# Hybrid attention, DeltaNet and PEER block: stores on the scalar engine's queue, three buffers for table rows, half of the gate columns made on VectorE, and dense rows pinned between the loop's steps

## The chip, the cores and the metric

The kernel runs on one core of a Trainium2 chip. The metric is device time in microseconds (us), the median of several executions. TensorE is called PE here, its weight loads PEld, VectorE DVE, ScalarE ACT, GpSimd POOL, and SyncE, which issues most transfers, SP.

## What is computed

One decoder layer on 512 tokens of width 1024: two mixers (sparse attention, gated DeltaNet), a merge, and then a retrieval layer (PEER) over 16384 single-neuron experts. The change touches only the PEER part, which the reference gives as:

```python
def peer(hn, w_query, sub_keys, u_tab, v_tab):
    q = (hf @ w_query).reshape(ntok, PEER_HEADS, 2, PEER_KEY_DIM // 2)
    s = jnp.einsum('nhpd,hpkd->nhpk', q.astype(f32), sub_keys.astype(f32))
    top_s, top_i = lax.top_k(s, PEER_TOPK)
    ...
    best_s, pos = lax.top_k(cand_s, PEER_TOPK)
    expert = jnp.take_along_axis(cand_i, pos, axis=-1)
    gate = jax.nn.softmax(best_s, axis=-1)
    ...
    def block(args):
        hb, eb, gb = args
        act = jax.nn.gelu(jnp.einsum('nhkd,nd->nhk', u_tab[eb], hb).astype(f32), approximate=False)
        coef = (gb * act).astype(hb.dtype)
        return jnp.einsum('nhk,nhkd->nd', coef, v_tab[eb])
```

Each token picks 8 x 16 = 128 experts of 128 x 128; for each it needs the product of its activation with a row of table u, a gelu, a gate, and a row of table v.

## The kernel before, in words

The program is written with a tile framework whose scheduler orders the instructions of each engine by a timeline of its own at build time; `tc.issue_after(ins)` (here `behind`, `held`) pins instructions of the same engine behind `ins`. Up to about 565 us the two mixers and the merge run, which the change leaves as they are. Then:

- **Scores and choice** (to about 832 us). Query projections and scores, then `choose(b)` for each of the four token blocks of 128, long runs of small DVE instructions that find the chosen experts and gates.
- **Dense u** (`dense_u(i)`, 128 table rows i of 128 experts each). For 320 of the 512 tokens (`NU`) the products with all experts are made: load `ut` (512 KB, two buffers), split it in a high and a low half (`uh` on ACT at line 174, `ul` on DVE at line 175), 24 matmuls of 128x320, and a gelu on ACT. The gelu's result stays in SBUF (`ge`, `AHEAD + 2` = 26 buffers) or, for the rows in `SPILLED` (60, set by `KEPT`), goes to DRAM (`gs`, line 836, issued by SP) and is loaded again later. 84 of the 128 rows (`first`: 24 kept ones and the 60 spilled) are made before the last loop, in step with the other work through `along`; the other 44 (`late`) in the last loop.
- **Gathered u and v**. Half of block 2 takes its u rows with 64 indirect DMAs of 512 KB (`ask`, line 977; product on DVE, line 992), and block 3 takes u and v rows with 128 indirect DMAs of 1 MB (`gathered`, line 998; product line 1006, sum into `x1g` line 1009). Both draw on the four `row` buffers.
- **Pieces** (`spread`, 24 pieces of 16 tokens, about 832 to 1152 us). For each token a matrix of gates over all experts is built as a product of two one-hot matrices: in two halves q of 8 tokens, DVE compares (`oa`, `ob`, line 1030), ACT scales each token's `ob` by its gates (line 1033, 8 instructions of 128x128), PE multiplies (two passes a token in the trace, 32 a piece), and ACT copies the sums of four tokens at a time into `gb` (line 1039). `gb` has one buffer of 1 MB and is stored to `gd` in DRAM (line 1041, issued by SP) in runs of 512 bytes.
- **The last loop** (`dense_v(i)` for 128 rows, about 1152 us to the end). Load `vt` (512 KB, two buffers), split it (`vh` on ACT, line 1127; `vl` on DVE, line 1128), multiply gates `gt` by the gelus (line 1131), split the product (`ch` on ACT, `cl` on DVE, two buffers each), and 18 matmuls of 128x512 that add to the accumulators `acc`. Gates for eight rows come in one load `gt` of 1.5 MB. About 120 of the gathers of block 3 are spread over the loop, paced by `vl`.

All matmuls stand under the helper's line 98, all splits under lines 174 and 175, all loads under line 109.

Of the kernel before, what the change touches and what calls it, by code (L numbers as in the profile page):

```python
# [19 lines left out]
P = 128  # L20
T = 512
D = 1024
# [26 lines left out]

AHEAD = 24  # L50
KEPT = 60
SPILLED = {i for i in range(P) if i * KEPT // P != (i + 1) * KEPT // P}

# [36 lines left out]
def tile_block(ctx, tc, x, xT, w_in, sc_cols, sc_rows, w_br, w_o, w_q, subT, uT, uv, cst, iota, out, dbg=None):  # L90
# [732 lines left out]
    def dense_u(i, a_):  # L823
        ut = up.tile([P, 8, P], F32, name="ut", bufs=2)
        load(ut, uT[i])
# [6 lines left out]
        if i in SPILLED:  # L832
            ge = up.tile([P, NU], F32, name="gs", bufs=2)
            gsd[i] = dr.tile([P, NU], F32, name=f"gs{i}")
            S.activation(ge, a_, AF.Gelu)
            nc.sync.dma_start(gsd[i], ge)
        else:
            ges[i] = up.tile([P, NU], F32, name="ge", bufs=AHEAD + 2)
            S.activation(ges[i], a_, AF.Gelu)
# [175 lines left out]
    def spread(b, gp):  # L1015
# [5 lines left out]
        for c in range(P // TC):  # L1021
            gb = gp.tile([P, P, TC], F32, name="gb", bufs=1)
            for q in range(TC // TB):
# [3 lines left out]
                ob = gp.tile([P, TB, P], F32, name="ob", bufs=2)  # L1027
                for i, o_ in enumerate((oa, ob)):
                    which = sl[:, i, n0:n0 + TB, None].to_broadcast([P, TB, P])
                    V.tensor_tensor(o_, io[:, None].to_broadcast([P, TB, P]), which, op=ALU.is_equal)  # L1030
                for t in range(TB):
                    n = n0 + t
                    S.activation(ob[:, t], ob[:, t], AF.Copy, scale=sl[:, 2, n:n + 1])  # L1033
                for g in range(TB // TG):
# [5 lines left out]
            dst = gd[:, :, b * (P // TC) + c, :].rearrange("g p k -> p g k")  # L1040
            nc.sync.dma_start(dst, gb.rearrange("p (g i) n -> p g (i n)", i=IC))
            yield
# [75 lines left out]
    def dense_v(i):  # L1118
# [3 lines left out]
        g = gts[i // IC][:, :, i % IC, :]  # L1122
        vt = ex.tile([P, D], F32, name="vt", bufs=2)
        load(vt, uv[i * P:(i + 1) * P, D:])
# [6 lines left out]
        V.tensor_tensor(gdn, activations(i).rearrange("p (c n) -> p c n", n=TC), gdn, op=ALU.mult)  # L1131
        ch = ex.tile([P, NCH, TC], F32R, name="ch", bufs=2)
        cl = ex.tile([P, NCH, TC], F32R, name="cl", bufs=2)
        split(ch, cl, g)
# [11 lines left out]
    for i in range(P):  # L1146
# [3 lines left out]
        if late and (total_u - len(late)) * (P - END) <= i * total_u:  # L1150
            dense_u(late.pop(0), ps3.tile([P, NU], F32, name="a_", bufs=2))
            spent += U_COST
# [73 lines left out]
```

## Time and profile before

| | |
|---|---|
| time, median of 3 runs | 1895.31 us (1889.37 to 1906.87) |
| profiled execution, its own time | 1899.46 us |
| its span, first to last instruction | 1897.7 us |
| mean granted TensorE clock | 0.98 of 2.4 GHz |
| busy, share of the span | PE 92%, PEld 80%, DVE 77%, ACT 48%, POOL 14% |
| moved by DMA | 433.77 MB, mean 229 GB/s |

The engines work side by side, so a busy share says little by itself. Matmuls are pipelined, and PE counts as busy while one is under way. What a stretch of the span is bound by is read from the chain of waits (which work ended last, followed back) and from what an engine waited for, stretch by stretch.

### The profile page before, as it was taken

Reading aid. Unit: us, or ns where it says so; the run is one execution under the profiler, and the core shown is the slowest. Engines: PE = TensorE matmul, PEld = TensorE weight load, DVE = VectorE, ACT = ScalarE, POOL = GpSimd, SP = SyncE. Lnnn points to the kernel's source line nnn. Section 1 sums busy time; section 2 is a strip of 40 time slices with the busy share of each in tenths; the row PEclk is TensorE's granted clock in tenths of the full one; section 3 lists DMA queues with packets and bytes.
Section 4 is the critical chain, followed back from the end, with each engine's and each line's share of the span. In section 5 each row is a group of like instructions: output and inputs, shape, how many; then the busy total and the mean of one; then the engine's idle time right before and its main releaser. Section 6 shows DMA issues by size and latency. Waiting matters only on the chain.

```text
span 1897.7 us, 26661 instructions
## 1 busy us (share of the span) xinstructions
PE 1754.7 (92%) x9527; PEld 1511.4 (80%) x9527; DVE 1463.5 (77%) x3084; ACT 912.4 (48%) x1787; POOL 270.8 (14%) x196
## 2 busy tenths in 40 slices
PE   6999999999999997888989898999999999789888
PEld 4787677777778897878988897888888888677666
DVE  5757988554766999988776776878878788789787
ACT  5533344434533343359977894434444443333333
POOL 0000000000000003430331102211111211222220
PEclk9999999999999999999999999999999999989999
DMA  4211111112633226877989799998989988989997
GB/s 148 85 68 67 45 45 58 60 45 85 210 128 122 79 103 258 296 244 217 298 282 310 248 291 334 359 356 320 346 329 337 343 333 319 349 329 359 343 343 254
DMA packets 155973, 433.77 MB, mean 229 GB/s; under 512 B 12480, under 2 KB 78144, under 8 KB 137408
## 3 DMA queue, kind: packets, MB, share of 16 engines
q1 hardware_dynamic: 128192, 264.28, 39.9%
q0 software_dynamic: 27648, 167.78, 23.8%
q8 instruction: 75, 1.23, 0.2%
q14 instruction: 58, 0.48, 0.1%
HBM read 388.73 MB, written 42.86 MB: 227 GB/s over the span
## 4 chain that ended last, share of the span: by engine, by line
PE 61%; DMA 15%; DVE 11%; ACT 8%; issue 4%; SPq 0%; DVEq 0%; ACTq 0%; POOL 0%; POOLq 0%
PE mm L98 21%; PE acc L98 19%; DMA vt<-in_uv_dram 6%; PE dn L98 5%; DMA gd<-gb 4%; PE wo L98 3%; DMA ut<-in_uT_dram 3%; PE at L98 3%; ACT gb L1039 3%; ACT ob L1033 2%; DVE ul L175 2%; DVE vl L1128 1%; ACT vh L1127 1%; DVE row L992 1%; ACT uh L174 1%
## 5 line engine op out<-in xcount | busy, mean ns | idle before, releaser
L98 PE MATMUL acc<-vl,ch 128*128 128x512 f32 x768 | 303.0, 395 | 2.3 <-DVE vl L1128 2.2
L98 PE MATMUL acc<-vh,cl 128*128 128x512 f32 x768 | 301.9, 393 | 0.0
L998 POOL DMA_INDIRECT row<-in_uv_dram,eidx x128 | 171.5, 1340 | 693.2 <-DVE x1g L1009 655.9
L98 PE MATMUL acc<-vh,ch 128*128 128x512 f32 x768 | 212.8, 404 | 42.5 <-ACT vh L1127 42.5
L98 PE MATMUL mm<-hTh,uh 128*128 128x320 f32 x672 | 217.9, 324 | 32.7 <-ACT uh L174 12.0
L98 PE MATMUL mm<-hTh,ul 128*128 128x320 f32 x672 | 218.4, 326 | 10.4 <-DVE ul L175 10.4
L977 POOL DMA_INDIRECT row<-in_uv_dram,eidh x64 | 99.1, 1548 | 901.0 <-DVE gate_g L913 730.0
L175 DVE TENSOR_TENSOR ul<-ut,uh 128x1024 fp32r<-128x1024 f32 x128 | 156.1, 1220 | 86.2 <-ACT uh L174 82.5
L98 PE MATMUL mm<-hTl,uh 128*128 128x320 f32 x672 | 214.3, 319 | 0.0
L98 PEld LDWEIGHTS acc<-vh,ch 128*128 128x128 f32 x768 | 144.5, 193 | 78.6 <-ACT vh L1127 51.2
L1128 DVE TENSOR_TENSOR vl<-vt,vh 128x1024 fp32r<-128x1024 f32 x128 | 156.4, 1223 | 50.6 <-ACT vh L1127 49.5
L174 ACT CAST uh<-ut 128x1024 fp32r<-128x1024 f32 x128 | 134.4, 1050 | 112.2 <-DMA ut<-in_uT_dram 51.0
L174 ACT CAST ch<-gt 128x384 fp32r<-128x384 f32 x128 | 65.6, 513 | 250.8 <-PE acc L98 246.6
L98 PEld LDWEIGHTS acc<-vl,ch 128*128 128x128 f32 x768 | 146.5, 191 | 34.7 <-DVE vl L1128 4.0
L98 PEld LDWEIGHTS acc<-vh,cl 128*128 128x128 f32 x768 | 145.8, 190 | 29.9
L1009 DVE SCALAR_TENSOR_TENSOR x1g<-row,co,x1g 128x1024 f32<-128x1024 f32 x128 | 163.8, 1280 | 5.5 <-ACT co L1008 3.5
L1127 ACT CAST vh<-vt 128x1024 fp32r<-128x1024 f32 x128 | 133.4, 1047 | 70.8 <-DMA vt<-in_uv_dram 70.1
L98 PEld LDWEIGHTS mm<-hTh,uh 128*128 128x128 f32 x672 | 131.5, 196 | 38.0 <-ACT uh L174 14.9
L1006 DVE CUSTOM_DVE_ANT_0 row<-row,h2g 128x1024 f32<-128x1024 f32 x128 | 154.6, 1219 | 0.9 <-DMA row<-in_uv_dram,eidx 0.9
L98 PE MATMUL mm<-hh,wh 128*128 128x512 f32 x344 | 144.6, 424 | 3.6 <-ACT hh L174 2.1
L98 PEld LDWEIGHTS mm<-hTh,ul 128*128 128x128 f32 x672 | 131.0, 195 | 13.2 <-DVE ul L175 13.1
L175 DVE TENSOR_TENSOR wl<-wt,wh 128x1024 fp32r<-128x1024 f32 (+1 forms) x81 | 90.1, 1115 | 63.5 <-ACT wh L174 63.2
(676 smaller groups left out, 3817.6 us busy)
## 6 DMA issues: line engine op xcount, KB each, us to landing
ut<-in_uT_dram SPq DMA_DIRECT2D x128, 512.0 KB
vt<-in_uv_dram SPq DMA_DIRECT2D x128, 512.0 KB
gd<-gb SPq DMA_DIRECT2D x24, 1024.0 KB
gt<-gd SPq DMA_DIRECT2D x16, 1536.0 KB
wt<-in_w_in_dram SPq DMA_DIRECT2D x43, 512.0 KB
gs<-gs SPq DMA_DIRECT2D x120, 160.0 KB
wt<-in_w_q_dram SPq DMA_DIRECT2D x16, 512.0 KB
sgd<-tmp SPq DMA_DIRECT2D x16, 256.0 KB
```

The source lines that it names most:

```text
L98: hop[0] = PE.matmul(o, l, r, start=start, stop=stop).ins
L174: S.copy(hi, src)
L175: return V.tensor_tensor(lo, src, hi.bitcast(F32), op=ALU.subtract).ins
L977: G.indirect_dma_start(out=asked[s // 2][:, s % 2], out_offset=None, in_=uv2, in_offset=bass.IndirectOffsetOnAxis(ap=eidh[:, s:s + 1], axi ...
L992: V.tensor_tensor_reduce(r, r, h2d, 1.0, 0.0, op0=ALU.mult, op1=ALU.add, accum_out=act[:, s:s + 1])
L998: G.indirect_dma_start(out=row.rearrange("p t d -> p (t d)"), out_offset=None, in_=uv, in_offset=bass.IndirectOffsetOnAxis(ap=eidx[:, s:s ...
L1006: V.tensor_tensor_reduce(row[:, 0], row[:, 0], h2g, 1.0, 0.0, op0=ALU.mult, op1=ALU.add, accum_out=a)
L1009: V.scalar_tensor_tensor(x1g, row[:, 1], co, x1g, op0=ALU.mult, op1=ALU.add)
L1033: S.activation(ob[:, t], ob[:, t], AF.Copy, scale=sl[:, 2, n:n + 1])
L1039: S.copy(gb[:, :, at:at + TG].rearrange("p i n -> p n i"), v4(p_))
L1127: S.copy(vh, vt)
L1128: paced = V.tensor_tensor(vl, vt, vh.bitcast(F32), op=ALU.subtract)
```

## The change

Gelu results (`gs`) and gate pieces (`gd`) are stored by DMAs that ACT issues instead of SP. `ut`, `vt`, `ch` and `cl` get a third buffer; `AHEAD` falls from 24 to 16 (18 buffers of `ge`) and `KEPT` rises from 60 to 68, so 68 rows are spilled; 84 rows still precede the loop and 44 are in it. In the second half (q = 1) of each piece the scaled one-hot matrix `ob` is made by eight DVE instructions of 128x128 (compare and multiply in one), in place of one compare of 128x1024 on DVE and eight scalings on ACT. In the loop a late `dense_u` is pinned on PE behind the last matmul of the `dense_v` before it.

```diff
-AHEAD = 24
-KEPT = 60
+AHEAD = 16
+KEPT = 68
...
-        ut = up.tile([P, 8, P], F32, name="ut", bufs=2)
+        ut = up.tile([P, 8, P], F32, name="ut", bufs=3)
...
-            nc.sync.dma_start(gsd[i], ge)
+            nc.scalar.dma_start(gsd[i], ge)
...
-                for i, o_ in enumerate((oa, ob)):
+                for i, o_ in enumerate((oa, ob)[:2 - q % 2]):
                     which = sl[:, i, n0:n0 + TB, None].to_broadcast([P, TB, P])
                     V.tensor_tensor(o_, io[:, None].to_broadcast([P, TB, P]), which, op=ALU.is_equal)
                 for t in range(TB):
                     n = n0 + t
-                    S.activation(ob[:, t], ob[:, t], AF.Copy, scale=sl[:, 2, n:n + 1])
+                    if q % 2:
+                        V.tensor_scalar(ob[:, t], io, sl[:, 1, n:n + 1], sl[:, 2, n:n + 1], op0=ALU.is_equal, op1=ALU.mult)
+                    else:
+                        S.activation(ob[:, t], ob[:, t], AF.Copy, scale=sl[:, 2, n:n + 1])
...
-            nc.sync.dma_start(dst, gb.rearrange("p (g i) n -> p g (i n)", i=IC))
+            nc.scalar.dma_start(dst, gb.rearrange("p (g i) n -> p g (i n)", i=IC))
...
-        vt = ex.tile([P, D], F32, name="vt", bufs=2)
+        vt = ex.tile([P, D], F32, name="vt", bufs=3)
...
-        ch = ex.tile([P, NCH, TC], F32R, name="ch", bufs=2)
-        cl = ex.tile([P, NCH, TC], F32R, name="cl", bufs=2)
+        ch = ex.tile([P, NCH, TC], F32R, name="ch", bufs=3)
+        cl = ex.tile([P, NCH, TC], F32R, name="cl", bufs=3)
...
-            dense_u(late.pop(0), ps3.tile([P, NU], F32, name="a_", bufs=2))
+            with behind(hop[0]):
+                dense_u(late.pop(0), ps3.tile([P, NU], F32, name="a_", bufs=2))
```

Since the scheduler orders anew, other instructions move too. On ACT, in one of the later pieces, the order before was:

```order
L1033 ACTIVATE ob<-ob,sl 128x128 x8
L174 CAST uh<-ut 128x1024
L835 ACTIVATE gs<-mm 128x320
L1033 ACTIVATE ob<-ob,sl 128x128 x8
L1007 ACTIVATE co<-a 128x1
L1008 ACTIVATE co<-co,gate_g 128x1
L835 ACTIVATE gs<-mm 128x320
L1039 COPY gb<-wo 128x4x128
L174 CAST uh<-ut 128x1024
L1039 COPY gb<-wo 128x4x128 x3
```

and in the changed kernel, with line 1036 for the scalings, 1042 for the copies and 1044 for the store, it is:

```order
L1007 ACTIVATE co<-a 128x1
L1008 ACTIVATE co<-co,gate_g 128x1
L174 CAST uh<-ut 128x1024
L835 ACTIVATE gs<-mm 128x320
L1036 ACTIVATE ob<-ob,sl 128x128 x8
L836 DMA gs_10423<-gs 128x320
L174 CAST uh<-ut 128x1024
L835 ACTIVATE gs<-mm 128x320
L1042 COPY gb<-wo 128x4x128
L836 DMA gs_10507<-gs 128x320
L1042 COPY gb<-wo 128x4x128 x3
L1044 DMA gd<-gb 128x16x128
```

One of the two blocks of eight scalings is gone, a cast no longer stands between the copies, and three issues of stores stand in ACT's stream, one of them between the copies.

At the end of the pieces ACT's order before kept two dense rows behind the last copies, and after the change (the second fence) the last two pieces have no dense row beside them:

```order
L1039 COPY gb<-wo 128x4x128
L174 CAST uh<-ut 128x1024
L1039 COPY gb<-wo 128x4x128 x3
L174 CAST uh<-ut 128x1024
L835 ACTIVATE gs<-mm 128x320
L174 CAST uh<-ut 128x1024
L835 ACTIVATE gs<-mm 128x320
L174 CAST uh<-ut 128x1024
```

```order
L1044 DMA gd<-gb 128x16x128
L174 CAST uh<-ut 128x1024
L835 ACTIVATE gs<-mm 128x320
L1036 ACTIVATE ob<-ob,sl 128x128 x8
L836 DMA gs_10923<-gs 128x320
L1042 COPY gb<-wo 128x4x128 x4
L1044 DMA gd<-gb 128x16x128
L1036 ACTIVATE ob<-ob,sl 128x128 x8
L1042 COPY gb<-wo 128x4x128 x4
L1044 DMA gd<-gb 128x16x128
L174 CAST ch<-gt 128x384 x3
```

What moved is dense rows, from the end of the pieces to their front. Counted over DVE's order, 36 dense rows (`ul`) and 28 products of line 992 stand ahead of the first `oa` before, and 41 and 32 now.

In the last quarter of the loop, SP's loads before were all for `dense_v`:

```order
L109 DMA vt<-in_uv_dram 128x1024 x4
L109 DMA gt<-gd 128x3072
L109 DMA vt<-in_uv_dram 128x1024 x2
L109 DMA gs<-gs_9965 128x320
L109 DMA gs<-gs_10000 128x320
L109 DMA vt<-in_uv_dram 128x1024 x2
```

and now loads of dense rows (`ut`) stand among them:

```order
L109 DMA vt<-in_uv_dram 128x1024 x2
L109 DMA ut<-in_uT_dram 128x1024
L109 DMA vt<-in_uv_dram 128x1024
L109 DMA gs<-gs_10042 128x320
L109 DMA gs<-gs_10126 128x320
L109 DMA vt<-in_uv_dram 128x1024 x2
L109 DMA ut<-in_uT_dram 128x1024
```

So loads of dense rows moved to the end of the loop. Before, the dense rows of the loop were made in its first 68 iterations, with single matmuls between those of `dense_v`; now one block of 24 stands after every second or third `dense_v`, to the end of the loop.

## Rows read from the trace of the kernel before

**Rows 1.** Busy time of each engine in four stretches of the span (choice, pieces, first and second part of the loop): stretch, its us, busy us with the number of instructions, granted clock, mean busy share of the 16 DMA engines, GB/s.

```profile
675.00:832.00 157.00, 133.77 (x842) 128.65 (x841) 147.34 (x540) 59.40 (x83) 49.54 (x35) 0.95 0.68 241
849.00:1152.00 303.00, 270.56 (x1889) 263.53 (x1888) 223.32 (x248) 254.82 (x569) 59.15 (x36) 0.96 0.86 276
1152.00:1590.00 438.00, 432.68 (x2255) 380.19 (x2254) 352.55 (x456) 189.88 (x355) 86.11 (x65) 1.00 0.91 340
1590.00:1898.00 308.00, 261.75 (x1080) 207.96 (x1079) 250.72 (x336) 112.90 (x228) 68.79 (x51) 0.95 0.88 328
```

**Rows 2.** The chain that ended last, shares by line, in the stretches 675 to 832, 832 to 1152 and 1590 to 1898 us.

```profile
by line: DVE ul L175 18.2%; DMA ut<-in_uT_dram 12.5%; PE mm L98 11.6%; DVE row L992 8.9%; issue 6.2%; DMA row<-in_uv_dram,eidh 4.8%; DVE oh L945 3.0%; DVE bp L908 2.9%; DVE bp L911 2.8%; ACT uh L174 2.7%; DVE cr L909 2.4%; DVE oh L946 2.2%; 
...
by line: DMA gd<-gb 26.5%; ACT gb L1039 15.3%; PE mm L98 13.2%; ACT ob L1033 11.5%; DMA ut<-in_uT_dram 8.5%; issue 7.0%; PE wo L98 6.1%; ACT uh L174 3.7%; DVE ob L1030 1.8%; DVE oa L1030 1.4%; ACT gs L835 1.1%; DVE row L992 1.1%; DVE ul L17
...
by line: DMA vt<-in_uv_dram 34.8%; PE acc L98 25.0%; issue 8.1%; DVE vl L1128 8.1%; ACT vh L1127 5.8%; DVE x1g L1009 4.0%; DMA gt<-gd 3.5%; DVE row L1006 3.2%; DVE gt L1131 2.4%; DVE cl L175 2.0%; ACT ch L174 0.7%; DVE xs L1164 0.4%; DVE a 
```

**Rows 3.** Who waited for whom between 1590 and 1890 us: us in total, times, longest.

```profile
ACT ch L174 <- PE acc L98: 90.6, 47, 3.6
ACT vh L1127 <- DMA vt<-in_uv_dram: 55.0, 28, 5.6
...
PE acc L98 <- ACT vh L1127: 38.5, 19, 6.1
```

**Rows 4.** The same between 1160 and 1590 us.

```profile
PE acc L98 <- ACT vh L1127: 4.0, 2, 2.7
```

**Rows 5.** Pieces of the chain between 832 and 1152 us in order of time: start, us, what.

```profile
864.30 5.19 DMA gd<-gb
...
875.66 5.34 DMA gd<-gb
...
919.44 9.47 DMA gd<-gb
930.96 2.23 ACT ob L1033 x8
936.28 5.67 DMA gd<-gb
...
1131.95 7.37 DMA ut<-in_uT_dram
1141.17 2.02 ACT gb L1039 x2
1143.20 8.88 DMA gd<-gb
```

**Rows 6.** Instructions on the tiles gb and act: line, engine, operation, count, ns (least, median, most), first and last start.

```profile
L1039 ACT COPY gb<-wo x96: 992/1093/1176, 839.2 to 1142.1; 128x512 f32<-128x512 f32 x96
L1041 SPq DMA_DIRECT2D gd<-gb x24: 370/371/378, 849.3 to 1143.2; - x24
...
L109 SPq DMA_DIRECT2D act_up<-act x1: 5895/5895/5895, 1035.5 to 1035.5; - x1
```

**Rows 7.** Two stores of gb by length: busy times and DMA in the 5.2 us of the store at 864.3 and the 9.5 us of the one at 919.4 (columns as in rows 1).

```profile
864.30:869.50 5.20, 5.20 (x41) 5.20 (x40) 4.38 (x7) 4.78 (x12) 0.00 (x0) 1.00 0.83 232
...
919.40:928.90 9.50, 9.50 (x73) 9.50 (x72) 7.89 (x9) 7.16 (x21) 1.96 (x1) 1.00 1.06 362
```

**Rows 8.** What SP issued next after the stores of 909.2 and 1143.2 us: start, us that the issue took, line, transfer.

```profile
909.64 2.12 SPq L836 DMA_DIRECT2D gs<-gs  x1
...
1144.39 4.74 SPq L836 DMA_DIRECT2D gs<-gs  x1
```

**Rows 9.** ACT's groups between 832 and 1152 us: busy us, mean ns of one, idle before.

```profile
L174 ACT CAST uh<-ut 128x1024 fp32r<-128x1024 f32 x50 | 52.6, 1051 | 15.9 <-DMA ut<-in_uT_dram 12.6 <-PE mm L98 3.3
L835 ACT ACTIVATE gs<-mm 128x320 f32<-128x320 f32 x45 | 19.9, 443 | 5.5 <-PE mm L98 3.0 <-issue 2.5
```

**Rows 10.** DVE's groups between 675 and 1152 us (columns as in rows 9).

```profile
L175 DVE TENSOR_TENSOR ul<-ut,uh 128x1024 fp32r<-128x1024 f32 x84 | 102.3, 1219 | 65.7 <-ACT uh L174 65.4
L992 DVE CUSTOM_DVE_ANT_0 row<-row,h2d 128x1024 f32<-128x1024 f32 x64 | 76.0, 1219 | 2.3 <-DMA row<-in_uv_dram,eidh 2.3
...
L1030 DVE TENSOR_TENSOR ob<-io,sl 128x1024 f32<-128x1024 f32 x48 | 58.5, 1219 | 0.0
...
L992 DVE DVE_READ_ACCUMULATOR2_ANT act<- 128x1 f32 x64 | 5.2, 82 | 0.0
...
L927 DVE TENSOR_SCALAR t<-bp 128x128 int32<-128x128 int32 x4 | 0.9, 218 | 0.0
```

**Rows 11.** The only group of DVE instructions with a column of scalars as operand and a compare-like form that is near in shape, by tile acc: ns (least, median, most) over the three shapes.

```profile
L533 DVE TENSOR_SCALAR acc<-R,small x3: 352/411/470, 117.6 to 242.7; 128x256 f32<-128x256 f32 x1, 128x384 f32<-128x384 f32 x1, 128x512 f32<-128x512 f32 x1
```

**Rows 12.** Pieces of the whole chain in which PE runs without a wait: 26 passes of the pieces' matmuls, 30 of `dense_v`, 24 of `dense_u`.

```profile
1124.28 2.90 PE wo L98 x26
...
1305.04 6.85 PE acc L98 x30
...
1371.61 3.52 PE a__14245 L98 x24
```

**Rows 13.** Three windows of the loop (columns as in rows 1).

```profile
1400.00:1450.00 50.00, 50.00 (x262) 44.00 (x262) 40.31 (x52) 21.34 (x39) 8.46 (x8) 1.00 0.95 361
...
1600.00:1650.00 50.00, 43.72 (x189) 34.69 (x187) 43.30 (x58) 18.60 (x40) 16.16 (x11) 1.00 0.91 348
...
1850.00:1898.00 48.00, 39.02 (x162) 31.09 (x161) 34.56 (x44) 14.61 (x30) 4.72 (x3) 0.93 0.71 253
```

## The prediction

> **What bounds the kernel now.** I read first the busy time by stretch, then the chain of waits inside each stretch, then who waited for whom. The part up to 675 us is built in the same order before and after, apart from one dense row, and is left out. Three stretches remain.
>
> *Choice, 675 to 832 us:* DVE is busy 147 of 157 us [rows 1], and the chain runs mostly over DVE, but 12.5% of it, 19.6 us, is waiting for the load `ut` [rows 2].
>
> *Pieces, 832 to 1152 us:* no engine is full (PE 271, ACT 255 of 303 us, rows 1). The chain is a cycle through the single buffer `gb`: its store is 26.5% of it, the copies into it 15.3%, the scalings on ACT 11.5%, and `ut` loads 8.5%, that is 27 us [rows 2]. The 24 stores are issued from 849.3 to 1143.2 us, one per 12.8 us [rows 6]. A cycle is a store and then the copies: 5.19 us and 6.2 us from 864.30 to 875.66, 9.47 and 7.4 us from 919.44 to 936.28, the second with eight scalings (2.23 us) among the copies [rows 5]. Stores come short or long: during the short one all traffic is 232 GB/s, during the long one 362, so the long ones share the engines with other transfers [rows 7].
>
> *The loop, 1152 to 1898 us:* two halves with different limits. To 1590 PE is busy 433 of 438 us, and waits for `vh` only 4.0 us; from 1590 PE is busy 262 of 308 us, waits 38.5 us for `vh`, which waits 55 us for the load `vt`, and `vt` is 34.8% of the chain [rows 1 to 4]. The reason is that all late dense rows were made in the first half.
>
> **The change part by part.**
>
> *1. Choice: more goes into it.* The built order puts 41 dense rows and 32 products ahead of the first `oa` where 36 and 28 stood. On DVE, which bounds here, that is 5 x 1.219 + 4 x (1.219 + 0.082) = 11.3 us [rows 10]. PE's 5 x 3.52 = 17.6 us fit in its 157 - 134 = 23 idle us [rows 1, 12]. Against it stands the third `ut` buffer, which can take away at most the 19.6 us of waiting; I take half. Sum: +1.5 us, between -8 and +11.
>
> *2. Pieces.* What is taken from ACT: eight scalings a piece; one block of eight took 2.23 us in a row [rows 5], so 24 x 2.2 = 53 us of ACT's time. What is added: the issues of 24 `gd` and of some 45 `gs` [rows 9], by SP's 0.37 and 0.33 us [rows 6, 8] 24 us. DVE gets eight instructions a piece for one of 1.219 us. An operation with two columns of scalars isn't in the trace; the nearest at 128x128 with fixed scalars takes 218 ns, and one with a column 352 ns at twice the width [rows 10, 11], so 24 x (8 x 0.218 - 1.22) = 13 us, at most 24 x (8 x 0.352 - 1.22) = 38 us. I take 13, for the shape is the same; DVE's 223 busy us of 303 hide it. If the cover is gone, it costs the difference of the two, 25 us.
>
> The store was not late before: SP stood waiting, and the store of 1143.20 followed the last copy at once [rows 5]. So the move to ACT doesn't bring the store forward; it frees SP. Behind a `gd` the next issue took 2.12 and 4.74 us [rows 8], and a `ut` load issued at 1131.95 needed 7.37 us [rows 5]. Now `ut` no longer queues behind the store, but may run beside it, and so lengthen it towards the 9.5 us of a shared one.
>
> A new cycle is therefore: store 7.0 us (short 5.3, long 9.5; I take a value between them that leans to the short, as only about two loads of 0.5 MB come per cycle), 0.3 to release ACT, four copies of 1.093 and the issues 0.33 and 0.37 in ACT's stream: 5.1 us [rows 6, 8]. That is 12.4 us. ACT's other work in the cycle (two casts and two gelus 3.0, one block of scalings 2.2, an issue) is 5.6 us and lies under the store [rows 5, 9]. PE needs 2 x 3.52 + 32 x 2.90/26 = 10.6 us and is not the limit [rows 12]. Twenty-one such cycles make 260 us; the last two, without a dense row beside them, store alone: 5.3 + 0.3 + 4.8 = 10.4 us each, 21 us. Before, one cycle was far longer: the piece for which block 2's gates must be ready waited for `act_up`, whose issue took 5.9 us behind a `gd` [rows 6]; SP is now free there, and I charge 4 us for what is left. Sum: 260 + 21 + 4 = 285 against 293.9: -9 us. With short stores throughout it is 21 x 10.7 + 25 = 250, -44; with long ones throughout 21 x 14.9 + 25 = 338, +44. Both ends are unlikely, as the stores before were mixed; for the range I take half of each, -22 to +22.
>
> The Trainium skill, "DMA: Bandwidth & Descriptors", section "Issuing engines are not separate DMA queues", says that issuing from several engines saves only the sequencer's time, usually small. In this trace that time is not small behind a `gd` [rows 8]. By the rule the pieces would give nothing, and the sum below would be 9 us worse.
>
> *3. The loop.* What it must move: 128 `vt` and 42 `ut` of 512 KB, 16 `gt` of 1.5 MB, 68 `gs` of 160 KB, some 120 gathers of 1 MB, and 3.7 MB at the end: 67.1 + 22.0 + 25.2 + 11.1 + 122 + 3.7 = 251 MB (the sizes follow from the tiles' shapes). Before it was about 250 MB in 746 us by the rates of rows 1; the eight rows more that are spilled add 1.3 MB here and as much in the pieces. What PE must do: 128 x 18 passes at 6.85/30 us and 42 blocks of 3.52 us: 526 + 148 = 674 us [rows 12]. So, spread evenly, both need about 5.3 us an iteration, and which ends last is open. Moving dense rows to the second half fills PE's idle 46 us there; the third buffers of `vt`, `ch` and `cl` take off both waits of rows 3. The question is the rate. Half one, with `ut` and `vt` in SP's queue, reached 361 GB/s in its best window, half two 348 [rows 13], and half one's mean was 340 with PE full. I take 357, near the best, for all but the last 48 us, whose drain at 253 GB/s (12 MB) remains: (251 - 12)/0.357 + 48 = 718 us against 746: -28 us. With half two's 348 it is 735, -11. With PE as the limit it is 674 us and about 16 for start and end (estimate): 690, -56. The pin costs something too: before, single dense matmuls filled PE's gaps; a block of 3.5 us can't be cut. I take nothing for it, since the waits it would cover in half one were 4.0 us [rows 4], at most the 38.5 us of half two, which would bring the loop back to +10.
>
> The Trainium skill, same page, section "Specifications", gives about 358 GB/s as the limit of HBM for a core. By it the loop could not end below (251 - 12)/0.358 + 48 = 716 us, and the second rival below would be out. The trace has one window at 361 [rows 13], so the rule is borne out as to size, not as a wall.
>
> **Sum.** 1.5 - 9 - 28 = -35.5 us on the profiled 1899.5: 1864. That execution lay 4.2 us over the median, so 1860 for the median.
>
> **The rivals.**
>
> *ACT is held by its own stores (slower).* An issue behind a `gd` blocked SP for 2 to 4.7 us [rows 8]. Now the `gs` issue behind a `gd` is ACT's, and behind it stand the cast `uh`, which PE's next dense row waits for, and the copies. In the later pieces ten instructions lie between the two, over 4 us, and little is left of the block; in the first eleven only a cast and a gelu, 1.5 us. From a stall of about 1.5 us a cycle ACT's 5.6 us exceed the store of 7 and every further us is on the path. With 4.7 us in each of 23 cycles it is 23 x 3.2 = 74 us more, less where the store is long anyway; with that 74, choice at +11, and the loop at -11, 1899.5 + 11 - 9 + 74 - 11 - 4.2 = 1960; in half of the cycles 1923. Against it: SP's blocks of over 2 us came right behind the `gd`, and ACT comes later.
>
> *PE becomes the limit of the loop (much faster).* If the third `vt` buffer keeps the transfers busy as never before, the loop takes 690 us; with the pieces at -9 the time is 1832. For it: PE without waits for 400 us in half one. Against it: no window before went over 361 GB/s, and this needs 239/0.642 = 372.
>
> *The loop stays at the rate of half two, and the pieces give nothing (no difference).* 1.5 + 0 - 11 = -9.5: 1886. For it: the DMA share is 0.91 and 0.88 in both halves [rows 1], as if transfers, not buffers, set the pace.
>
> **How the numbers follow.** This kernel's measurement can tell about 1% from no change. Forecast 0.48, around 1860; PE-bound loop 0.16; no difference 0.23; slower 0.13. Faster by over 1% (under 1876) takes the second and nearly all of the first: 0.61; within 1% takes the third and the slow tail of the forecast: 0.27; slower by over 1%: 0.12, the first rival. The range, 1826 to 1897, holds the second and third cases and the bounds of the loop, and leaves the slow rival out.
>
> **What would show it.** Right: PE busy about equally in all windows of the loop, no wait of `vh` for `vt` above a few us, over 350 GB/s in its middle; store-to-store time of about 12.4 us in the pieces, 10.4 in the last two; first store some us later than before. Wrong: `gs` issues on ACT of several us and `uh` behind them; stores of 9 us throughout; PE waiting for `vh` all along the loop at 348 GB/s; DVE's new instructions over 0.3 us; a fall of the granted clock from 1.0 in the loop, where it is 1.00 and 0.95 now [rows 1].

## The result, and the profile after

The changed kernel takes 1846.97 us (median of 4 runs, 1843.05 to 1852.02), 0.9733 of the kernel before, with an interval of 0.968 to 0.9785 (the four runs of the kernel before that stand beside it have a median of 1897.82). Forecast were 1860 us and a range of 1826 to 1897. The profiled execution took 1847.1 us, its span 1845.3 against 1897.7. One of the four executions of experiment 2 took 5509 us and is left out of the time and the ratio given there.

Busy time by stretch of the changed kernel (columns as in rows 1; the first two stretches answer to the first two of rows 1, and the last line is the whole loop):

```profile
675.00:853.00 178.00, 160.26 (x1049) 155.00 (x1048) 171.46 (x595) 78.09 (x112) 62.02 (x40) 0.98 0.72 259
853.00:1126.00 273.00, 245.03 (x1757) 241.41 (x1755) 238.66 (x401) 203.76 (x382) 61.58 (x36) 0.97 0.90 294
...
1140.00:1340.00 200.00, 197.36 (x969) 170.10 (x970) 176.04 (x235) 86.68 (x169) 53.31 (x35) 0.99 0.95 364
1340.00:1540.00 200.00, 193.34 (x948) 165.10 (x947) 170.20 (x224) 84.75 (x166) 42.05 (x33) 1.00 0.95 360
1540.00:1740.00 200.00, 194.63 (x964) 167.16 (x963) 171.36 (x223) 86.78 (x169) 46.92 (x34) 1.00 0.93 355
1140.00:1839.80 699.80, 683.81 (x3359) 587.05 (x3360) 598.27 (x783) 297.19 (x578) 161.33 (x116) 1.00 0.92 350
```

In the pieces ACT is busy 204 us where it was 255, and PE 245 of 273 where it was 271 of 303. In the loop the two halves of before are gone: PE is busy at 97 to 99% in each of the three windows, and the transfers run at 355 to 364 GB/s. PE lacks 16 us in the whole loop; in the second part alone it lacked 46 before [rows 1].

The table below splits the span. "First store" and "pieces" go by the issues of the 24 `gd` stores, "loop" goes from the first to the last matmul on `acc`, and the length of a store goes from its issue to its last packet (mean of the 24 in the packet records). "Copies" is the time from the first of a piece's four copies to the issue of its store.

| | first store | pieces | last store to loop | loop | store | copies |
|---|---|---|---|---|---|---|
| before | 849.3 | 294.0 | 19.2 | 730.2 | 6.40 | 5.50 |
| after | 853.2 | 272.5 | 14.3 | 700.3 | 7.05 | 3.89 |
| difference | +3.9 | -21.5 | -4.9 | -29.9 | +0.65 | -1.61 |

The stretches sum to -52.4 us. (The 5 us behind the loop are the same in both.) Each stretch is read from one execution. The four kernels of experiments 2 to 5, which differ from the change in the loop alone, have pieces of 268.4 to 280.6 us and first stores at 849.1 to 853.7 us, so a few us in these two columns say nothing.

The chain by line of the pieces (853 to 1126 us) and of the loop (1140 to 1840), which answer to rows 2:

```profile
by line: PE mm L98 32.3%; PE wo L98 23.3%; DMA gd<-gb 22.6%; ACT gb L1042 12.2%; issue 4.9%; ACTq L836 2.4%; ACT gs L835 1.3%; DVE oa L1030 0.9%; ACT ob L1036 0.6%; DVE oh L946 0.4%; ACTq L1044 0.4%; DVE ob L1034 0.4%; PE tr L1018 0.1%; ACT
```
```profile
by line: PE acc L98 73.1%; ACT vh L1130 1.6%; issue 1.0%; DMA ut<-in_uT_dram 0.8%; PE a__10980 L98 0.5%; PE a__11130 L98 0.5%; PE a__11276 L98 0.5%; PE a__11426 L98 0.5%; PE a__11572 L98 0.5%; PE a__11712 L98 0.5%; PE a__11862 L98 0.5%; PE 
```

In the pieces the waits for `ut` and the scalings on ACT, 8.5 and 11.5% of the chain before, are gone or below 1%, and PE holds 56% of the chain. In the loop the load `vt` is gone from the chain, and PE is nearly all of it.

Who waited for whom in the loop (answers to rows 3 and 4: us in total, times, longest):

```profile
ACT ch L174 <- PE acc L98: 228.9, 119, 3.6
...
PE acc L98 <- ACT vh L1130: 34.0, 13, 18.2
```

The longest of PE's waits, 18.2 us, is the one ahead of the loop's first matmul. 15.8 us are left in 12 waits, where there were 42.5 in 21 [rows 3, 4]. `vh` waited for the load `vt` for 1.9 us in all.

The tiles `gb`, `ob` and `act_up` (answers to rows 6):

```profile
L1042 ACT COPY gb<-wo x96: 1012/1126/1196, 849.3 to 1124.6; 128x512 f32<-128x512 f32 x96
L1044 ACTq DMA_DIRECT2D gd<-gb x24: 377/377/379, 853.2 to 1125.6; - x24
...
L1036 ACT ACTIVATE ob<-ob,sl x192: 384/389/415, 845.7 to 1119.2; 128x128 f32<-128x128 f32 x192
L1034 DVE TENSOR_SCALAR ob<-io,sl x192: 329/340/534, 846.0 to 1119.8; 128x128 f32<-128x128 f32 x192
...
L109 SPq DMA_DIRECT2D act_up<-act x1: 467/467/467, 1010.2 to 1010.2; - x1
```

The new DVE instruction takes 340 ns. The issue of `act_up` takes 0.47 us, where it took 5.9.

Pieces of the chain from 875 to 945 us (start, us, what; answers to rows 5), and under it the traffic during the two stores in it (answers to rows 7):

```profile
875.08 3.02 ACT gb L1042 x3
878.12 7.79 DMA gd<-gb
...
886.87 3.03 ACT gb L1042 x3
889.91 0.38 ACTq L1044
...
891.83 2.80 ACTq L836
...
925.17 2.99 ACT gb L1042 x3
...
928.20 14.19 DMA gd<-gb
```
```profile
928.20:942.40 14.20, 11.10 (x73) 10.84 (x72) 11.54 (x21) 5.38 (x13) 5.50 (x4) 0.88 1.02 356
...
878.10:885.90 7.80, 7.80 (x61) 7.73 (x60) 7.80 (x15) 5.10 (x12) 0.98 (x1) 1.00 1.00 314
```

Three copies take 3.0 us in a row. The issue of `gs` behind a store (line 836) holds ACT for 2.80 us here. The store of 7.8 us had 314 GB/s of traffic in all, the one of 14.2 us 356; its own 1 MB makes up 134 and 74 GB/s of that. In the second one PE was busy for only 11.1 of the 14.2 us, and its granted clock was 0.88 of 2.4 GHz.

### The profile page after: what moved, and what is told of

The parts are those of the page before. It is cut to its first block, busy times and chain, and to the rows that moved or that the text cites. A ratio compares the mean times of both kernels' runs of the same rounds, so it can differ in the third digit from the quotient of the medians.

```text
span 1845.3 us, 26570 instructions
## 1 busy us (share of the span) xinstructions
PE 1732.1 (94%) x9527; PEld 1501.4 (81%) x9527; DVE 1484.1 (80%) x3252; ACT 860.0 (47%) x1595; POOL 285.1 (15%) x196
## 4 chain that ended last, share of the span: by engine, by line
PE 78%; DVE 8%; DMA 5%; ACT 5%; issue 2%; ACTq 0%; DVEq 0%; SPq 0%; POOL 0%; POOLq 0%
PE acc L98 28%; PE mm L98 26%; PE wo L98 6%; PE dn L98 5%; DMA gd<-gb 3%; PE at L98 3%; ACT gb L1042 2%; DVE ul L175 2%; DVE row L992 1%; PE tr L98 1%; ACT vh L1130 1%; PE at L578 0%; PE dn L327 0%; DVE tmp L236 0%; DMA wt<-in_w_br_dram 0%
## 5 line engine op out<-in xcount | busy, mean ns | idle before, releaser
L998 POOL DMA_INDIRECT row<-in_uv_dram,eidx x128 | 186.0, 1453 | 653.9 <-DVE x1g L1009 611.5
L98 PE MATMUL acc<-vh,ch 128*128 128x512 f32 x768 | 227.5, 394 | 34.0 <-ACT vh L1130 34.0
L98 PE MATMUL mm<-hTh,uh 128*128 128x320 f32 x672 | 212.1, 316 | 19.8 <-ACT gs L835 16.9
L98 PE MATMUL mm<-hTh,ul 128*128 128x320 f32 x672 | 207.4, 315 | 9.0 <-DVE ul L175 8.7
L98 PE MATMUL mm<-hTl,uh 128*128 128x320 f32 x672 | 209.3, 311 | 0.0
L174 ACT CAST ch<-gt 128x384 fp32r<-128x384 f32 x128 | 65.5, 514 | 242.3 <-PE acc L98 228.9
L1131 DVE TENSOR_TENSOR vl<-vt,vh 128x1024 fp32r<-128x1024 f32 x128 | 156.3, 1221 | 18.5 <-ACT vh L1130 17.6
L98 PEld LDWEIGHTS mm<-hTh,uh 128*128 128x128 f32 x672 | 127.8, 190 | 23.0 <-ACT gs L835 19.5
L98 PE MATMUL mm<-hh,wl 128*128 128x512 f32 x344 | 137.1, 400 | 0.0
L98 PE MATMUL mm<-hl,wh 128*128 128x512 f32 x344 | 136.8, 398 | 0.0
## 6 DMA issues: line engine op xcount, KB each, us to landing
gt<-gd SPq DMA_DIRECT2D x16, 1536.0 KB, 10.7
```

The lines of the kernel that those rows point to most:

```text
L98: hop[0] = PE.matmul(o, l, r, start=start, stop=stop).ins
L174: S.copy(hi, src)
L998: G.indirect_dma_start(out=row.rearrange("p t d -> p (t d)"), out_offset=None, in_=uv, in_offset=bass.IndirectOffsetOnAxis(ap=eidx[:, s:s ...
L1131: paced = V.tensor_tensor(vl, vt, vh.bitcast(F32), op=ALU.subtract)
```

## The experiments

Two questions were open. **The loop:** does its gain come from the pin, which spreads the dense rows over both halves, or from the third buffers; and from which? **The pieces:** they gained more than forecast; which of the three edits (stores on ACT, gate columns on DVE, third `ut`) gives it, and do ACT's blocked issues cost what the first rival said? All stretches below are read as in the table above, and each ratio is against the kernel before.

### 1. The pin alone, on the kernel before

```
-            dense_u(late.pop(0), ps3.tile(...))
+            with behind(hop[0]):
+                dense_u(late.pop(0), ps3.tile(...))
```

> The kernel before with one edit: each late dense row of the loop is pinned on PE behind the matmuls of the dense_v before it; all buffers, stores and counts stay. Theory A (the loop got faster because dense rows are spread over all of it, so PE and transfers are both needed evenly): the stretch from the first to the last matmul into acc falls from 729.8 us to 700 to 712, the time to about 1875. Rival B (the third buffers of vt, ch and cl did it, by feeding the transfers better): the stretch stays at 720 to 732, since two buffers of vt still hold the loads back, and the time at 1890 or above.

Measured: 1888.77 us, 0.9935 (0.9912 to 0.9958). The loop took 721.4 us against 730.2; the pieces did not change (293.3). Windows of the loop and the wait for the load, 1165 to 1800 us:

```profile
1190.00:1390.00 200.00, 189.58 (x905) 161.53 (x904) 163.56 (x213) 82.65 (x159) 44.60 (x32) 0.97 0.91 343
1390.00:1590.00 200.00, 190.34 (x919) 161.42 (x917) 164.47 (x219) 83.05 (x159) 43.57 (x33) 0.98 0.91 346
1590.00:1790.00 200.00, 193.18 (x955) 165.90 (x956) 170.30 (x220) 86.75 (x167) 46.25 (x34) 1.00 0.94 353
```
```profile
ACT vh L1127 <- DMA vt<-in_uv_dram: 48.8, 33, 4.1
```

The work is now spread evenly, as the prediction wanted it, and still `vh` waits 48.8 us for `vt`, in 33 times; in the same stretch of the kernel before it was 49.4 us in 33. The wait has only been spread too. The pin gives 9 us of loop, not the 30 of the whole change.

### 2. The change without the pin

```
-            with behind(hop[0]):
-                dense_u(late.pop(0), ps3.tile(...))
+            dense_u(late.pop(0), ps3.tile(...))
```

> The changed kernel without the pin: late dense rows may run ahead again, third buffers stay. Theory A: PE is full in a first part and idle in a second again, the stretch of acc goes from 699.8 us back to 718 or more, the time to about 1866. Rival B: the third vt buffer lets the transfers of the second part go faster than the 348 GB/s of before, the stretch stays under 706 and the time under 1853.

Measured: 1844.14 us, 0.9707 (0.9653 to 0.9761): as fast as with it. The loop took 695.7 us against 700.3, but its first matmul comes 20.7 us behind the last store where it came after 14.3. Its windows:

```profile
1190.00:1390.00 200.00, 199.29 (x1038) 175.09 (x1037) 161.90 (x207) 84.89 (x162) 42.66 (x31) 1.00 0.91 339
1390.00:1590.00 200.00, 197.64 (x999) 171.11 (x998) 167.41 (x218) 86.13 (x166) 51.80 (x33) 1.00 0.91 341
1590.00:1790.00 200.00, 180.34 (x776) 143.28 (x775) 178.83 (x243) 80.15 (x165) 57.63 (x39) 1.00 0.97 375
```

The dense rows stand in the first part again, and PE is full there. In the last window, where no `ut` is loaded any more, the transfers now run at 375 GB/s, and PE has 180 busy us in 200. In the kernel before, whose dense rows stand in the first part too, the same window was:

```profile
1590.00:1790.00 200.00, 171.77 (x711) 137.14 (x711) 167.77 (x229) 75.26 (x154) 48.57 (x36) 0.95 0.90 340
```

So dense rows in the second half are not what the loop needed, and with the other edits in place the pin has no effect that can be told from none.

### 3. The change with two buffers of `vt`, `ch` and `cl`

```
-        vt = ex.tile([P, D], F32, name="vt", bufs=3)
+        vt = ex.tile([P, D], F32, name="vt", bufs=2)
```
and the same for `ch` and `cl`.

> The changed kernel with two buffers of vt, ch and cl instead of three; the pin stays. Theory A: the stretch of acc grows by under 8 us (to 700 to 707), the time is under 1856. Rival B: it grows by 15 us or more, waits of vh for vt come back to above 30 us, and the time is 1862 or more.

Measured: 1859.2 us, 0.9799 (0.9739 to 0.9859). The loop took 717.9 us, 17.6 more, and the pieces 271.5, as before the edit. The wait for the load between 1165 and 1800 us is back:

```profile
ACT vh L1130 <- DMA vt<-in_uv_dram: 53.8, 33, 6.7
```

That is close to the loop of the pin alone (721.4): with the pin and two buffers of all three tiles the loop takes 718 to 721 us, whatever else was changed ahead of it.

### 4. Only `vt` with two buffers

> The changed kernel with two buffers of vt; ch and cl keep three. Theory G (the third vt buffer took away the wait for loads, which was 9.0% of the chain of the loop with two of all): the stretch of acc goes from 700.3 us to 713 to 720, the time to about 1860. Rival H (ch and cl: the cast ch waits for PE on ACT's stream and the cast vh stands behind it): the stretch stays under 705 us.

Measured: 1880.79 us, 0.9863 (0.9831 to 0.9895). The loop took 734.2 us, 34 more than with three and above both expectations. Between 1165 and 1800 us:

```profile
ACT vh L1130 <- DMA vt<-in_uv_dram: 75.2, 41, 5.8
...
PE acc L98 <- ACT vh L1130: 34.9, 17, 4.2
```

So `vt`'s third buffer carries the loop's gain. How much it is worth depends on what stands beside it: 34 us here, 23 us between experiments 3 and 5 (717.9 and 695.3). Why two buffers of `vt` with three of `ch` and `cl` do worse than two of each (734 against 718) stays open. Of the 42 us by which this trace is longer than the change's, 8 stand in the pieces (280.6 us against 272.5), which the edit doesn't touch; that too is open. The profiled execution was the longest of the four, 8.4 us over their median.

### 5. Only `ch` and `cl` with two buffers

> The changed kernel with two buffers of ch and cl, three of vt. With two of vt the stretch of acc was 734 us, with two of all 718, with three of all 700. If vt alone matters, it stays at 697 to 705 us and the time at 1842 to 1851; if the third ch and cl are needed with it, 710 us or more.

Measured: 1839.18 us, 0.9666 (0.9613 to 0.9719). The loop took 695.3 us. The third `ch` and `cl` give nothing. With three of them ACT's cast `ch` still waited 228.9 us in the loop for matmuls on `acc`. Those only read `ch`, so the wait is for a buffer to come free; it costs nothing where PE is full.

### 6. All stores back on SP

```
-            nc.scalar.dma_start(gsd[i], ge)
+            nc.sync.dma_start(gsd[i], ge)
-            nc.scalar.dma_start(dst, gb.rearrange(...))
+            nc.sync.dma_start(dst, gb.rearrange(...))
```

> The changed kernel with both stores (gs, gd) issued by SP again. Theory C (freeing SP lets loads of dense rows start early, and that shortened the pieces): the time from the first to the last store of gb goes from 272.4 us to 282 or more, with waits of uh for ut of above 10 us, and the time to about 1858. Rival D (who issues doesn't matter; the scalings moved to DVE and the dense rows moved ahead of the pieces shortened them, and ACT's own blocked issues cost about what SP's did): it stays at 268 to 276, and the time at 1843 to 1851.

Measured: 1833.11 us, 0.9642 (0.9596 to 0.9688), 14 us better than the change by the medians. The pieces took 257.9 us against 272.5; the loop did not change (701.7). The store lasts 6.32 us on the mean against 7.05. The chain of the pieces, 852 to 1110 us, the stores, and the wait of the copies for the store, here and (last fence) in the change:

```profile
by line: PE mm L98 44.4%; PE wo L98 26.7%; ACT gb L1042 4.9%; DMA gd<-gb 4.5%; DVE row L992 4.0%; issue 2.7%; DVE ul L175 2.7%; DMA gs<-gs 2.6%; DVE oa L1030 1.9%; DVE ob L1034 1.7%; ACT ob L1036 1.6%; ACT uh L174 1.2%; DVE ob L1030 0.9%; A
```
```profile
L1044 SPq DMA_DIRECT2D gd<-gb x24: 370/371/371, 852.0 to 1109.9; - x24
```
```profile
ACT gb L1042 <- DMA gd<-gb: 26.1, 13, 4.6
```
```profile
ACT gb L1042 <- DMA gd<-gb: 19.3, 10, 4.5
```

The store falls from 22.6% of the chain to 4.5%, and PE holds 71% of it. A piece takes 257.9 / 23 = 11.2 us, near the 10.6 us that PE needs for two dense rows and 32 products. So with the stores on SP the pieces are bound mostly by PE, and moving the stores to ACT is what kept the change from it. Two of the change's stores, of 13.8 and 14.8 us, make cycles of 18.2 and 19.1 us; the same two pieces take 14.7 and 13.3 us here, and that is 9 of the 14.6 us. The copies themselves sit idle for the store no less than in the change, so this wait alone doesn't tell the two kernels apart; only the chain does. No cast waits for `ut` here, so theory C falls; rival D falls too, since the pieces got shorter than its range.

### 7. Only the `gs` stores back on SP

```
-            nc.scalar.dma_start(gsd[i], ge)
+            nc.sync.dma_start(gsd[i], ge)
```

> The changed kernel with the stores of gs issued by SP again, those of gd still by ACT. With both on SP the time from the first to the last store of gb was 257.9 us, with both on ACT 272.5. Theory E (ACT itself is held: its 50 issues of gs in the pieces took 47.3 us, about 31 more than 0.33 us each): without them on ACT the pieces fall to 256 to 262 us though the stores of gb still average about 7.0 us. Rival F (a store of gb on a queue of its own runs beside more loads and lasts longer, 7.05 against 6.32 us): the pieces stay at 267 to 274.

Measured: 1852.46 us, 0.9737 (0.9717 to 0.9757): no better than the change. The pieces took 276.9 us, the store 7.46 us. In this kernel no `gs` issue stands behind a store on ACT, and it is not faster. The chain, 851 to 1129 us, and the wait of the copies from 855 to 1100 us:

```profile
by line: DMA gd<-gb 31.0%; ACT gb L1042 18.6%; PE mm L98 12.1%; PE wo L98 11.3%; issue 5.5%; DVE row L992 3.5%; DVE oa L1030 3.3%; ACT ob L1036 2.8%; DVE ob L1034 2.6%; DVE ul L175 2.5%; ACT uh L174 2.3%; DVE ob L1030 1.7%; ACT gs L835 1.4%
```
```profile
ACT gb L1042 <- DMA gd<-gb: 43.7, 12, 13.5
```

So taking ACT's blocked issues away, 45 us summed over the 43 between the first and the last store of the changed kernel and up to 6.1 us each, does not shorten the pieces. With ACT free, what holds them is the `gd` store, which the next copies wait for, since `gb` has one buffer: three stores took 10.0, 13.0 and 19.7 us. The pieces lie a little above rival F's range, within the spread given under the table.

### 8. A second `gb` for the change

```
-            gb = gp.tile([P, P, TC], F32, name="gb", bufs=1)
+            gb = gp.tile([P, P, TC], F32, name="gb", bufs=2)
```

> The changed kernel with a second buffer of gb, the stores still on ACT's queue. If the long store (7.05 us on the queue of its own) costs time only because ACT waits for the one buffer, the pieces fall from 272.5 to 250 to 260 us, where PE's 10.6 us a piece end last, and the waits of the copies for the store vanish. If the slower store hurts by what it takes from the loads beside it, they stay at 266 or more.

Measured: 1836.52 us, 0.9668 (0.9612 to 0.9724). The pieces took 261.8 us, 10.7 less, between what the two sides expected. No copy waits for a store any more, while the stores themselves last 7.70 us. So a part of what the store costs goes through the single buffer. It is not all of it. Experiment 12 has a second `gb` too, with the stores on SP and without the pin, and its pieces take 250.5 us. With one buffer the stores on ACT cost 14.6 us of pieces (experiment 6), with two buffers still 11.3, though no copy waits for a store in either; the pin does little to the pieces (258.5 us without it, 257.9 with it, stores on SP). The 43 issues of `gs` hold ACT for 43.2 us here, up to 5.1 us each; whether they are that rest stays open, as no kernel with two buffers and only the `gs` stores on SP was run. The pieces (columns as in rows 1):

```profile
850.80:1112.60 261.80, 243.84 (x1753) 240.80 (x1751) 237.68 (x400) 204.12 (x381) 59.45 (x36) 0.97 0.92 306
```

### 9. All scalings on ACT again

```
-                for i, o_ in enumerate((oa, ob)[:2 - q % 2]):
+                for i, o_ in enumerate((oa, ob)):
...
-                    if q % 2:
-                        V.tensor_scalar(ob[:, t], io, ...)
-                    else:
-                        S.activation(ob[:, t], ob[:, t], AF.Copy, ...)
+                    S.activation(ob[:, t], ob[:, t], AF.Copy, ...)
```

> The changed kernel with all scalings of ob on ACT again, as before. Theory I (the second block of scalings stood among the copies into gb and lengthened the cycle): from first copy to store 3.9 us becomes 5 or more, the pieces 290 to 300 us and the time 1862 or more. Rival J (ACT had room; it is the earlier loads and dense rows that shortened the pieces): the pieces stay under 280 us.

Measured: 1886.08 us, 0.9905 (0.9886 to 0.9924). The pieces took 311.6 us, 39 more. Who waited, 855 to 1100 us:

```profile
DVE ul L175 <- ACT uh L174: 46.9, 16, 8.4
...
PE wo L98 <- ACT ob L1033: 25.7, 9, 8.7
```

PE waits for the scalings, and DVE for the cast `uh`, which stands behind ACT's other work. The gate columns on DVE are worth 39 us here, more than the whole gain of the pieces: without them the other edits together leave the pieces 17.6 us longer than before (294.0). How much of these 17.6 us is the stores on ACT was not run.

### 10. Two buffers of `ut`

```
-        ut = up.tile([P, 8, P], F32, name="ut", bufs=3)
+        ut = up.tile([P, 8, P], F32, name="ut", bufs=2)
```

> The changed kernel with two buffers of ut. The built order then puts 36 dense rows ahead of the first oa in place of 41, and the last two pieces have dense rows beside them again. Theory K (the third buffer let dense rows fill PE's idle time in the choice): the first store of gb comes 2 to 6 us earlier, the pieces take 284 us or more, with waits of uh for ut above 10 us, the time is 1853 or more. Rival L (it only shifts work): what the pieces lose the choice gains, and the time stays at 1843 to 1851.

Measured: 1882.66 us, 0.9897 (0.9877 to 0.9917). The pieces took 308.9 us, 36 more, and the loop 699.7, no more. The built order moves with the buffer: in the trace 35 dense rows stand ahead of the first `oa` (36 before the change), where 41 do in the change. Between the first and the last store PE makes 1848 matmuls where it made 1755, four blocks of 24 and some 14 us of PE's work (estimate, at 3.52 us a block). So the 36 us are those of the buffer and of the order that came with it, and the run does not part them. The chain, 845 to 1155 us:

```profile
by line: DMA gd<-gb 20.5%; ACT gb L1042 16.0%; PE mm L98 12.8%; PE wo L98 10.6%; issue 7.5%; ACTq L836 6.6%; ACT uh L174 6.3%; ACT ob L1036 4.8%; DMA act_up<-act 3.0%; DVE oa L1030 2.4%; ACT gs L835 2.1%; DMA ut<-in_uT_dram 1.8%; DVE ob L10
```

PE falls to 23% of the chain, and ACT's blocked issues (`ACTq L836`) rise from 2.4 to 6.6%, 20 us. So with less room for dense rows the first rival's stall does come out on the path.

### 11 and 12. Stores on SP and no pin; the same with a second `gb`

The first takes the edits of experiments 2 and 6, the second that of 8 as well.

> The changed kernel without the two edits that gained nothing: stores on SP's queue, no pin in the loop. If they add up: pieces 254 to 260 us, stretch of acc 694 to 703 us, time 1824 to 1834. If the pin pays once stores are on SP: stretch of acc above 706, time above 1836.

> The kernel c_sp_nopin with a second buffer of gb. With stores on SP the chain of the pieces was 71% PE and 4.5% the store, so little is left: pieces 248 to 257 us, time 1820 to 1832. If the single buffer still holds the copies, 245 us or less and a time under 1818.

Measured: 1836.61 us, 0.966 (0.9607 to 0.9713), and 1825.05 us, 0.9602 (0.9548 to 0.9657). The first has the pieces of experiment 6 (258.5) and a loop of 697.6 us, but its first matmul on `acc` comes 20.8 us behind the last store, where it came after 14.5; together it gives nothing over experiment 6, and the time lies above the 1834 us expected. The second has the shortest pieces of all, 250.5 us, and a loop of 696.0, and is the fastest kernel of the study, 22 us under the change. Its pieces:

```profile
851.40:1101.90 250.50, 238.21 (x1766) 236.26 (x1766) 237.27 (x400) 201.83 (x381) 64.52 (x36) 0.99 0.97 320
```

PE and DVE are busy 238 and 237 of 250.5 us, and the DMA engines 97%. In experiment 8 PE was busy 5.6 us longer, with no more matmuls, at a granted clock of 0.97 where it is 0.99 here; that is half of the 11.3 us between the two.

## Why the prediction was right, and where its steps were not

The sign held, the range held, and the sum was 13 us too high. Two of the reasons were wrong: the edit that was to help the pieces by freeing SP costs time there, and the one that was to help the loop gives nothing that shows. Others carry the gain, so that the forecast came as near as it did is in part luck. Two of its signs of being wrong came true without the time suffering: `gs` issues of up to 6.1 us on ACT, and DVE's new instructions at over 0.3 us.

**Choice** (+1.5 forecast, +3.9 measured). The first `oa` starts 11.2 us later (831.4 and 842.6), and 11.3 was the sum of DVE's work. The 9.8 us that the third `ut` buffer was to take off failed: DVE was idle for only 10 of these 157 us [rows 1], so the 19.6 us of `ut` on the chain were not time that DVE could gain. They are gone from the chain (675 to 853 us), PE's matmuls stand there in their place, and the first `oa` comes no earlier:

```profile
by line: PE mm L98 25.3%; DVE ul L175 17.7%; DVE row L992 10.5%; issue 6.0%; DMA row<-in_uv_dram,eidh 3.9%; DVE bp L908 3.4%; DVE oh L948 2.7%; DVE oh L945 2.6%; DVE oh L946 2.6%; DVE bp L911 2.6%; ACT uh L174 2.1%; DVE cr L909 1.8%; ACT L8
```

7.3 us came back elsewhere: from the first `oa` to the first store it is 10.6 us where it was 17.9. That the small sum was near is luck.

**Pieces** (-9 forecast, -21.5 measured). Four terms:

- The *store* was forecast at 7.0 us and measured at 7.05, as a mean of 4.7 to 14.8.
- The *copies with their issues* were forecast at 5.1 us and took 3.9. This is the term that failed in size. The sum added up the copies one behind the other at 1.09 us each, and three of them take 3.0 us in a row; the issues were added too, and ran where they were not in the way. 23 cycles at 1.2 us are 28 us; not half of it came out.
- The *DVE instruction* was forecast at 218 ns with a bound of 352; it took 340. The nearest in shape was the wrong choice, the nearest in form (with a column of scalars) the right one. It cost nothing all the same: DVE is busy 239 of 273 us.
- *The blocked issue of `act_up`* went, as forecast (5.9 to 0.47 us); the 4 us charged for what would be left were not needed.

The sum closes like this: 21 cycles took 12.1 us on the mean where 12.4 were forecast, the last two 9.4 and 9.0 where 10.4 were, and the 4 us fell away, 6.3 + 2.4 + 4 = 12.7 us. The cycles are near the forecast although their store and copies add up to 1.2 us less, because the work of another engine ended last in many of them: PE, set aside at 10.6 us a cycle as "not the limit", holds 56% of the chain. That the scalings would leave the cycle was right, and experiment 9 puts it at 39 us.

The reason was wrong at the step "Behind a `gd`...": the prediction counted the move of the stores to ACT as what frees SP and the `ut` loads. Experiment 6 shows that the move costs 14 us, and experiment 8 with 12 that a second `gb` does not take that cost away. SP did remain blocked in experiment 6 (a `ut` issue behind a store took 1.6 to 5.6 us), but with three `ut` buffers nobody waits for it. The third `ut` buffer and the gate columns on DVE carry the gain, 36 and 39 us each if taken away, so that with the stores on ACT neither does it without the other; with the stores on SP neither was taken away.

The passage on the Trainium skill, "DMA: Bandwidth & Descriptors", section "Issuing engines are not separate DMA queues", set the rule against the pieces' gain: another issuing engine saves only the sequencer's time. In direction the trace agrees: the move gave no gain (experiments 6 and 7). What the prediction made of the rule, that the pieces give nothing, did not follow, since other edits brought their gain. The trace shows a queue of their own for the stores on ACT, q10, which the kernel before does not have, beside SP's q1 (packets, MB, share of 16 engines; the changed kernel):

```profile
q1 hardware_dynamic: 71168, 230.59, 34.6%
...
q10 hardware_dynamic: 59328, 36.31, 6.4%
```

**The loop** (-28 forecast, -35 measured; 30 of it lie between the first and the last matmul on `acc`, the rest between the last store and the first of them). The size was near, and the step behind it fell: "Moving dense rows to the second half fills PE's idle 46 us there". Experiment 1 has that alone, and it gives 9 us; experiment 2 leaves it out, and loses nothing. The third `vt` buffer does it: with it the wait of `vh` for `vt` is gone (1.9 us in the change), and the transfers run at 355 to 364 GB/s where the dense rows are spread, and at 375 where none are left (experiment 2, last window; 340 before). In the first two windows of experiment 2, where PE is full, they stay at 339 and 341. The prediction named the third buffers in the same sentence but gave the 46 us to the moved rows.

The terms of the rate came out close. The forecast's stretch begins 8.8 us behind the last store, in the changed kernel at 1134.4; from there to the end (forecast 718 us) the trace has

```profile
1797.30:1845.30 48.00, 42.92 (x207) 36.37 (x205) 34.01 (x44) 13.96 (x30) 3.81 (x3) 0.98 0.56 207
1134.40:1845.30 710.90, 684.36 (x3360) 587.18 (x3360) 603.12 (x792) 299.47 (x582) 161.33 (x116) 0.99 0.92 350
...
1134.40:1797.30 662.90, 641.43 (x3155) 550.81 (x3156) 569.11 (x749) 285.51 (x553) 157.51 (x113) 0.99 0.94 360
```

710.9 us: 360 GB/s where 357 was taken, and 248.6 MB (663 us at 360 and 48 at 207) where 251 was. PE's work is 684 us, forecast 674, and it is without work for 27 us, forecast 16. So PE's work is 96% of the time, and the same bytes at the 375 GB/s of the best window would be 93% (estimate); the chain names PE. The second rival's loop (690 us, at 372 GB/s) did not come.

Of the 358 GB/s that the Trainium skill gives (same page, section "Specifications"): windows of 200 us at 364 and 375 GB/s stand above it by 2 and 5%, so as a size it is borne out, as a wall not. The Trainium skill says further down on the same page (section "Measured (HBM→SBUF, 128 partitions, SWDGE, issued from GpSimd)") that each core gets about this much when both cores of a pair stream. This kernel runs on one core, so by the page the figure was no reason to leave the second rival out.

**The pin's cost** was taken as nothing; 4.6 us of loop separate experiment 2 from the change, and 6.4 us of lead-in the other way, with times that can't be told apart.

**The rivals.** *ACT is held by its own stores:* the blocked issues are there, 14 of them over 0.9 us, but 2.4% of the pieces' chain is all that they hold; experiment 7 takes them away and gains nothing. In the order of experiment 10 they hold 6.6% of it, and with a second `gb` their cost is open (experiment 8). *PE becomes the limit of the loop:* the chain there is PE's, but at the forecast's rate, 21 us longer than this rival said; with the stores on SP, PE becomes the limit of the pieces as well. *No difference:* the DMA shares of 0.91 and 0.88 [rows 1] were not the transfers' limit, for the same loop reaches 0.93 to 0.97 in windows.

**Open:** why a `gd` store lasts longer on ACT's queue (6.61 to 7.46 us in the change and experiments 2 to 5 and 7) than on SP's (6.32 and 6.33, experiments 6 and 11); with a second `gb` it is 7.70 and 7.14. The long ones have other traffic beside them, 356 GB/s in the one of 14.2 us; on SP's queue the loads wait behind the store instead. That fits, but no experiment took the loads away by themselves. And the length is not the whole cost: the shortest pieces of all (experiment 12) have stores of 7.14 us, longer than the change's.

## What to carry to other kernels

Give a third buffer to the load that the chain of waits names, before reordering work around it: here that was 23 to 34 us, and the reordering at most 9. Before moving a store to another engine's queue, run the move by itself: here it cost 14 us of the pieces with one buffer and some 11 with two, in a change that was faster as a whole. Take a time off an engine's path only as far as that engine was idle. An issue that blocks its engine costs only what the next reader of that engine misses: look whether it is on the chain before charging its microseconds.

## What the hardware showed that was not expected

- A store issued by ACT has a queue of its own in the trace (q10), and an issue behind a store of 2048 packets of 512 B holds ACT for up to 6.08 us (0.33 us when free).
- Copies on ACT of 1.1 us each, back to back, take 1.0 us apiece: three in 3.0 us.
- DVE's compare-and-multiply with two columns of scalars takes 340 ns at 128x128, the form with fixed scalars 218, on whole numbers [rows 10].
- One core moved 364 GB/s (the change) and 375 GB/s (experiment 2) over 200 us.
